# Weight sums of an MLP made in HBM instead of on VectorE, and begun two at a time behind loads in attention

## The chip, the cores and the metric

The kernel runs on one core of a Trainium2 chip. Its time is the device time of one execution in microseconds (us). Of the engines, TensorE (PE) multiplies matrices, VectorE (DVE) and ScalarE (ACT) work elementwise, GpSimd (POOL) works elementwise and issues DMAs of its own, and SyncE (SP) here only issues DMAs. Each of these takes its instructions strictly in program order; semaphores order them against each other.

## The reference

One layer of a decoder trunk on x of 1 x 512 x 1024 in float32: two token mixers side by side (a pooling mixer, and sparse attention with 16 heads of 64), merged by sigmoid gates and projected back, and then an MLP with a hidden width of 4096. The part that the change touches is the MLP:

```
x = x + mixers(rms_norm(x))                       # attention, pooling, gates, w_out
h = rms_norm(x)
x = x + square(relu(h @ w_ff1)) @ w_ff2           # 1024 -> 4096 -> 1024
out = rms_norm(x)
```

## The kernel before

The program is one long, unrolled sequence in three stages: input projections and attention (0 to some 370 us), the projection back (to some 460 us), and the MLP (to the end).

*The MLP.* The hidden width goes in four chunks of 1024 (c = 0 to 3). In a chunk there is a first product (layer 1, with `w_ff1`) and a second (layer 2, with `w_ff2`). Each is done with seven products of quarters in place of eight, after Winograd: a weight block falls into quarters A11, A12, A21, A22, and the weights that PE needs are A11, A12, A22 and four sums, S1 = A21 + A22, S3 = A11 + A21, S2 = S1 + A11 (first product) or S3 + A22 (second), and S4 = S2 + A12; the signs are in what they are multiplied with. Each block has two groups, g = 0 and 1, so that one weight is 128 x 1024 elements, 512 KB. Names carry layer, chunk and group: S2_231 is S2 of layer 2, chunk 3, group 1; S4_231 the S4 of the same.

*A weight's way.* SP loads it (`emit_load`, line 233) into one of five buffers `raw`; ScalarE rounds it to its upper part `wh` or `w3h` (line 304); VectorE makes the rest `wl` or `w3l` (line 306); PE multiplies in three combinations of upper and lower parts (line 1398 in the first product, line 1515 in the second). The second product's order of weights is A11 A11 S1 S1 S3 A12 S3 A12 A22 A22 S2 S4 S2 S4, groups in turn. A22 is added onto the banks of PSUM that held S3's product, once VectorE has taken that off into x (line 1539, two instructions for the two halves); so the first half of A22's first group waits for the first of the two, and its second half for the second.

*The sums.* Most sums are made in HBM before they are loaded: SP copies one quarter to a place in HBM (`make_sum`, line 263), and POOL issues a DMA that adds another quarter onto it (`add_sum`, line 271). Where a sum starts from another sum, the copy has to wait until that one's addition has landed; SP stands there, and the loads behind it too. The list `jobs` fixes the order of the sums. Before, one sum is begun behind each load from three loads behind the first phase on to the projection back, and behind every third load in the MLP (`sums_after`). The other sums are made on VectorE: a buffer is held, and the next weight is added onto it (line 316; line 294 for S4 of the second product). In the second product of chunks 0 to 2, S2 is S3 plus A22 on VectorE, for which S3's buffer is held until A22 is there. In chunk 3 both S2 and S4 are made in HBM.

*Attention.* POOL multiplies the attention weights P by a column sm (line 1078, tiles of 128x128 to 128x512), and PE then turns them (line 1095, result psT). The additions of sums that begin here stand among those on POOL. The "fillers" are the loads of the gate and projection weights that attention's matmuls are interleaved with.

Of the kernel before, what the change touches and what calls it, by code (L numbers as in the profile page):

```python
# [62 lines left out]
def trunk(ctx: ExitStack, tc: tile.TileContext, A, out):  # L63
# [41 lines left out]
    def add_key(k):  # L105
# [14 lines left out]
        else:  # L120
# [4 lines left out]
    P1 = ("ck ks u0 wk0 wk1 u1 wk2 u2 kw wk3 cv u3 V0 V1 V2 wv0 q0 wv1 ga0 wv2 wpool q1 wv3 ga1 q5 "  # L125
          "ga2 q2 pp0 q6 pp1 q7 pp2 q3 pp3 q4").split()
    FILL2 = "gb0 gb1 gb2 ga3 gb3 ga4 gb4 ga5 gb5 ga6 gb6 ga7 gb7".split()
# [8 lines left out]
    MLP0 = len(LD)  # L136
# [6 lines left out]
    jobs, late = [], []  # L143

    def quarters(layer, c, g):

        if layer == 2:
            return {f"{i + 1}{j + 1}": w_f2[1024 * c + 512 * j + 256 * g:1024 * c + 512 * j + 256 * g + 256,
                                            512 * i:512 * i + 512].rearrange("(k p) c -> p k c", p=128)
                    for i in range(2) for j in range(2)}  # L150
        o = 1024 * c + 512 * g
        return {f"{i + 1}{j + 1}": w_f1[512 * j:512 * j + 512, o + 256 * i:o + 256 * i + 256].rearrange(
            "(k p) c -> p k c", p=128) for i in range(2) for j in range(2)}

    def add_group(layer, c, g):

        q = quarters(layer, c, g)
        of = {"A" + k: v for k, v in q.items()}
        final = layer == 2 and c == LAST
        for o in ("S1", "S3", "S2", "S4")[:4 if final else 4 - layer]:  # L160
            of[o] = dp.tile(list(q["11"].shape), F32, name=f"{o}_{layer}{c}{g}")
        jobs.append((of["S1"], q["21"], q["22"]))
        jobs.append((of["S3"], q["11"], q["21"]))
        if late:
            jobs.append(late.pop())
        if layer == 1:
            late.append((of["S2"], of["S1"], q["11"]))
        if final:
            jobs.append((of["S2"], of["S3"], q["22"]))
            jobs.append((of["S4"], of["S2"], q["12"]))  # L170
        return of

    SUM_OF, PLUS = {}, {}
    SUMS = {"S2": "S4", "A12": "S4"}, {"S3": "S2", "A22": "S2", "S2": "S4"}

    def add_turn(layer, c, of, turn):
        for g, o in turn:
            key = f"{o}{layer}{c}{g}"
            to = SUMS[layer - 1].get(o) if "S4" not in of[g] else None
            if to:  # L180
# [10 lines left out]
    for c in range(4):  # L191
        of = [add_group(1, c, g) for g in range(2)]
        if c == 0:
            turn = [(g, o) for os in FIRST[:1] for o in os for g in range(2)]
            turn += [(g, o) for os in FIRST[1:] for g in range(2) for o in os]
        else:
            turn = [(g, o) for g in range(2) for o in IN_TURN]
        add_turn(1, c, of, turn)
        of = [add_group(2, c, g) for g in range(2)]
        seen = {}  # L200
        turn = []
        for o in OUT_TURN if c < LAST else [o for o in LAST_TURN for g in range(2)]:
            g = seen.get(o, 0)
            seen[o] = g + 1
            turn.append((g, o))
        add_turn(2, c, of, turn)
# [7 lines left out]
    def emit_load():  # L214

        i = st["load"]
        if i >= len(LD):
            return False
        segs = LD[i]
        a = segs[0][0].shape[1]  # L220
        b = sum(s.shape[2] for s, _ in segs)
        assert a * b <= 1024
        if not by_name() or st["kept"] < RAW:
            st["kept"] += by_name()
            t = wp.tile([128, 1024], F32, tag="raw", bufs=RAW, name=f"raw{i}")
        elif spare:
            t = spare.pop(0)
        else:
            return False
        st["load"] += 1  # L230
        v = t[:, :a * b].rearrange("p (a b) -> p a b", a=a)
        for s, o in segs:
            began = nc.sync.dma_start(v[:, :, o:o + s.shape[2]], s)
        raws[i] = (t, a, b)
        if sums_after(i):
            make_sum(began)
        if i >= len(P1) + len(FILL2) + 4 and (len(begun) > 2 or begun and st["sums"] == len(jobs)):
            add_sum()
        return True

    def sums_after(i):

        if i < MLP0:
            return len(P1) + 3 <= i < len(P1) + len(FILL2) + 8
        return i % 3 == 0

    def by_name():

        return st["load"] >= MLP0

    def give_back(*tiles):
        spare.extend(tiles)
        while spare and by_name() and emit_load():
            pass

    def make_sum(load):

        if st["sums"] < len(jobs):
            to, q, _ = jobs[st["sums"]]
            while any(q is jobs[n][0] for n in begun):  # L260
                add_sum()
            with tc.issue_after(load.ins):
                nc.sync.dma_start(to, q)
            begun.append(st["sums"])
            st["sums"] += 1

    def add_sum(behind=None):

        to, _, q = jobs[begun.popleft()]
        with tc.issue_after(behind.ins) if behind else nullcontext():  # L270
            POOL.dma_start(to, q, accum_op=ALU.add)  # L271
# [15 lines left out]
    def group_steps(i):  # L287

        key, at = WL[i]
        if i in PLUS:  # L290
            while st["load"] <= PLUS[i]:
                assert emit_load()
            t = raws.pop(PLUS[i])[0]
            DVE.tensor_tensor(t, t, held[key], op=ALU.add)
            give_back(held.pop(key))
            yield
        elif isinstance(at, str):
            t = held.pop(key)
        else:
            while st["load"] <= at:  # L300
                assert emit_load()
            t = raws.pop(at)[0]
# [134 lines left out]
    def fm_halves(keys, psp, posts, tag, xT):  # L437

        ws, ps = [], []
        for h in range(2):  # L440
            tok = slice(256 * h, 256 * h + 256)
            for i, k in enumerate(keys):
                if h == 0:
                    ws.append(use(k))
                    ps.append(psp.tile([128, S], F32, tag=tag[0], bufs=tag[1], name="psF"))
                prods = fm_products(ws[i][0], ws[i][1], xT, tok=tok)
                if h == 0:
                    prods = prods[0::3] + prods[2::3] + prods[1::3]
                for j, (a, b) in enumerate(prods):
                    last_mm[0] = PE.matmul(ps[i][:, tok], a, b, start=h == 0 and j == 0,  # L450
                                           stop=h == 1 and j == len(prods) - 1, skip_group_check=True)
                    if j % 12 == 11:
                        ahead()
                        step_side()
                if h == 1:
                    r = posts[i](ps[i])
                    if r is not None:
                        side.append(r)
                yield
# [91 lines left out]
    def evac0(i, after=None):  # L551
        sl = slice(128 * i, 128 * i + 128)
        for a in range(2):
            ks = slice(4 * a, 4 * a + 4)
            r = ACT.activation(hT[0][:, ks, sl], trs[i][a], AF.Copy)
            with behind(after) if after else nullcontext():
                v = DVE.tensor_tensor(hT[1][:, ks, sl], trs[i][a], hT[0][:, ks, sl].bitcast(F32), op=ALU.subtract)
        return r, v
# [8 lines left out]
    r, _ = evac0(1)  # L567
# [9 lines left out]
    first = fm_halves(("ck", "ks"), ps1, (lambda ps: first_posts[0](ps), lambda ps: first_posts[1](ps)), ("F", 2), hT)  # L577
# [95 lines left out]
    with ExitStack() as c1:  # L673
# [187 lines left out]
        for k in P1[2:]:  # L861
            i = int(k[-1]) if k[-1].isdigit() else None
# [710 lines left out]
    def out_of(t):  # L1573
        return MA[:, 2 * t:2 * t + 2, :].rearrange("p j c -> p (j c)")
# [48 lines left out]
    for f in range(2):  # L1623
        t = 2 + f
        o = out_of(t)
# [26 lines left out]
    o, r = out_of(3), sq[:, 3, 4:5]  # L1652
# [23 lines left out]
```

## Time and profile before

| | |
|---|---|
| time, median of 3 runs | 792.52 us (790.69 to 794.8) |
| the profiled execution | 793.79 us |
| its span, first to last instruction | 792.0 us |
| PE busy in the span | 774.8 us, 98% |
| VectorE, ScalarE, POOL busy | 619.3, 488.6, 179.5 us |
| loads of raw weights from w_ff | 54 |
| loads of sums, copies from w_ff, copies from a sum, additions | 44, 32, 12, 44 |

The profiled execution is one run; it stands 1.27 us above the median. A row of the timeline has the start in us, the duration, the engine, the line of the kernel, the operation, result <- operands by name, shape, and how many; in square brackets how long the engine had been idle before, and what ended that. An engine called SPq is SP's queue of DMA issues: the duration there is the issue, not the transfer. Matmuls of 512 columns are drawn 0.39 us long and start some 0.23 us apart, since PE's pipeline overlaps them.

### The profile page before, as it was taken

Reading aid. Unit: us, or ns where it says so; the run is one execution under the profiler, and the core shown is the slowest. Engines: PE = TensorE matmul, PEld = TensorE weight load, DVE = VectorE, ACT = ScalarE, POOL = GpSimd, SP = SyncE. Lnnn points to the kernel's source line nnn. Section 1 sums busy time; section 2 is a strip of 40 time slices with the busy share of each in tenths; the row PEclk is TensorE's granted clock in tenths of the full one; section 3 lists DMA queues with packets and bytes.
Section 4 is the critical chain, followed back from the end, with each engine's and each line's share of the span. In section 5 each row is a group of like instructions: output and inputs, shape, how many; then the busy total and the mean of one; then the engine's idle time right before and its main releaser. Section 6 shows DMA issues by size and latency. Waiting matters only on the chain. (4 is left out here: it accounts for less than half of the span.)

```text
span 792.0 us, 12823 instructions
## 1 busy us (share of the span) xinstructions
PE 774.8 (98%) x4541; PEld 674.1 (85%) x4541; DVE 619.3 (78%) x1177; ACT 488.6 (62%) x962; POOL 179.5 (23%) x245
## 2 busy tenths in 40 slices
PE   8999999999999999999999999999999999999995
PEld 6889877888888888988888899879997999789974
DVE  6888666445999888887656489997899789878897
ACT  6756543335988888896334485934783478247745
POOL 4000000025876666673100000111110110110002
PEclk9999999999999999999999999999999999999998
DMA  9554733487753434335956508989998996978552
GB/s 309 134 152 120 198 108 100 127 213 185 135 108 80 99 90 107 80 81 93 346 145 216 130 1 243 327 205 298 260 289 227 281 285 198 279 227 259 165 181 107
DMA packets 116154, 142.33 MB, mean 180 GB/s; under 512 B 5525, under 2 KB 88121, under 8 KB 115898
## 3 DMA queue, kind: packets, MB, share of 16 engines
q1 hardware_dynamic: 97690, 117.72, 45.8%
q0 software_dynamic: 18112, 23.07, 19.2%
q10 hardware_dynamic: 288, 0.72, 0.3%
q8 instruction: 36, 0.59, 0.3%
q14 instruction: 28, 0.23, 0.1%
HBM read 136.77 MB, written 48.23 MB: 234 GB/s over the span
## 5 line engine op out<-in xcount | busy, mean ns | idle before, releaser
L393 PE MATMUL psF<-R,wh 128*128 128x512 f32 x512 | 164.4, 402 | 0.0
L304 ACT ACTIVATE wh<-raw 128x1024 fp32r<-128x1024 f32 x75 | 79.2, 1058 | 85.7 <-PE psB L1515 32.1
L271 POOL DMA_DIRECT2D S<-w_ff x44 | 48.7, 1107 | 360.3 <-DMA S<-w_ff 286.1
L350 ACT ACTIVATE wh<-raw 128x512 fp32r<-128x512 f32 (+1 forms) x100 | 60.3, 620 | 85.3 <-PE psF L393 43.3
L306 DVE TENSOR_TENSOR wl<-raw,wh 128x1024 fp32r<-128x1024 f32 x75 | 92.2, 1231 | 23.4 <-ACT wh L304 23.4
L393 PEld LDWEIGHTS psF<-R,wh 128*128 128x128 f32 x512 | 92.1, 188 | 17.9
L393 PE MATMUL psF<-R,wl 128*128 128x512 f32 x256 | 101.3, 396 | 0.0
L1078 POOL TENSOR_SCALAR P<-P,sm,GT 128x128 f32<-128x128 f32 (+3 forms) x128 | 83.1, 671 | 55.2 <-DVE sm L1068 38.7
L352 DVE TENSOR_TENSOR wl<-raw,wh 128x512 fp32r<-128x512 f32 (+1 forms) x85 | 58.6, 696 | 26.3 <-ACT wh L350 26.2
L1062 ACT ACTIVATE P<-P,sm 128x128 f32<-128x128 f32 (+3 forms) x128 | 71.1, 559 | 9.9 <-DVE sm L1052 9.2
L1052 DVE CUSTOM_DVE_ANT_0 P<-psS,cst 128x128 f32<-128x128 f32 (+3 forms) x128 | 59.7, 483 | 8.4 <-PE psT L1095 5.3
L1398 PE MATMUL psB<-R,wh 128*128 128x256 f32 x352 | 64.1, 282 | 0.0
L304 ACT ACTIVATE w3h<-raw 128x1024 fp32r<-128x1024 f32 x37 | 39.1, 1055 | 36.3 <-PE psB L1398 14.1
L1110 DVE TENSOR_TENSOR PT<-psT,PT 128x512 fp32r<-128x512 f32 (+2 forms) x96 | 56.6, 596 | 3.5 <-ACT PT L1106 2.9
L393 PEld LDWEIGHTS psF<-R,wl 128*128 128x128 f32 x256 | 48.1, 188 | 11.3
L1106 ACT ACTIVATE PT<-psT 128x512 fp32r<-128x512 f32 (+2 forms) x96 | 49.5, 520 | 8.8 <-PE psT L1095 7.8
L1398 PEld LDWEIGHTS psB<-R,wh 128*128 128x128 f32 x352 | 54.3, 189 | 0.5 <-DVE R L1340 0.2
L306 DVE TENSOR_TENSOR w3l<-raw,w3h 128x1024 fp32r<-128x1024 f32 x37 | 45.8, 1238 | 9.2 <-ACT w3h L304 9.2
L1095 PE MATMUL psT<-ident,P 128*128 128x128 f32 x320 | 50.9, 273 | 0.9 <-DVE PT L1110 0.9
L1398 PE MATMUL psB<-R,wl 128*128 128x256 f32 x176 | 49.5, 281 | 0.0
L1095 PEld LDWEIGHTS psT<-ident,P 128*128 128x128 f32 x320 | 39.4, 140 | 9.7 <-issue 1.8
L1129 PE MATMUL psO<-PT,VV 128*128 128x256 f32 x320 | 47.7, 286 | 0.0
(381 smaller groups left out, 2001.8 us busy)
## 6 DMA issues: line engine op xcount, KB each, us to landing
raw<-w_ff SPq DMA_DIRECT2D x54, 512.0 KB, 6.1
S<-w_ff POOLq DMA_DIRECT2D x44, 512.0 KB, 7.5
raw<-S SPq DMA_DIRECT2D x44, 512.0 KB, 5.0
raw<-w_in SPq DMA_DIRECT2D x32, 512.0 KB, 4.1
S<-w_ff SPq DMA_DIRECT2D x32, 512.0 KB, 7.1
S<-S SPq DMA_DIRECT2D x12, 512.0 KB, 5.3
raw<-w_proj_nsa SPq DMA_DIRECT2D x8, 512.0 KB, 4.4
raw<-w_out SPq DMA_DIRECT2D x8, 512.0 KB, 4.5
```

The lines of the kernel that those rows point to most:

```text
L304: ACT.activation(h, t, AF.Copy)
L306: DVE.tensor_tensor(l, t, h.bitcast(F32), op=ALU.subtract)
L350: ACT.activation(h[:, sl], t[:, sl], AF.Copy)
L352: eng.tensor_tensor(l[:, sl], t[:, sl], h[:, sl].bitcast(F32), op=ALU.subtract)
L393: PE.matmul(ps, a, b, start=first and j == 0, stop=last and j == n - 1, skip_group_check=True)
L1052: DVE.tensor_tensor_reduce(out=P[:, o:o + n].rearrange("p (a c) -> p a c", c=128), in0=s, in1=m, scale=1.0, scalar=3e38, op0=ALU.add, op1= ...
L1062: last_exp[:] = [ACT.activation(c, c, AF.Exp, bias=sm[:, 0, e:e + 1], scale=-1.0, accum_out=sm[:, 1, e:e + 1])]
L1078: r = POOL.tensor_scalar(P[:, o:o + n], P[:, o:o + n], sm[:, 2, e:e + 1], GT[:, qb, c + e:c + e + 1], op0=ALU.mult, op1=ALU.mult)
L1095: PE.transpose(pt[:, 128 * j:128 * j + 128], P[:, 128 * j:128 * j + 128], ident)
L1106: ACT.activation(dH, src, AF.Copy)
L1110: DVE.tensor_tensor(dL, src, dH.bitcast(F32), op=ALU.subtract)
L1398: PE.matmul(out, w[u][:, k, 128 * f:128 * f + 128], XB[x][v][:, k, :], **kw)
```

## The change

Two edits. First, in the second product of chunks 0 to 2, S2 is no longer S3 plus A22 on VectorE but a sum made in HBM like the others (a copy of S3, to which A22 is added). There are 50 sums in HBM in place of 44; 18 of them are copies of another sum, in place of 12. Six additions at line 316 go, and six loads of raw weights come, since S2 has its own load. S3 and A22 are not held any longer. S4 of these products stays on VectorE. As in layer 1, S2 of a group stands in `jobs` one group later than its S3, by way of `late`.

Second, `sums_after` gives a number: from the tenth load behind the first phase to the fourth behind the last filler, two sums are begun behind each load. With it 26 sums are begun ahead of the MLP where 18 were, and 24 in the MLP where 26 were.

```diff
--- before.py
+++ after.py
@@ add_group @@
-        for o in ("S1", "S3", "S2", "S4")[:4 if final else 4 - layer]:
+        for o in ("S1", "S3", "S2", "S4")[:4 if final else 3]:
...
         if layer == 1:
             late.append((of["S2"], of["S1"], q["11"]))
+        if layer == 2:
+            late.append((of["S2"], of["S3"], q["22"]))
         if final:
-            jobs.append((of["S2"], of["S3"], q["22"]))
+            jobs.append(late.pop())
             jobs.append((of["S4"], of["S2"], q["12"]))
...
-    SUMS = {"S2": "S4", "A12": "S4"}, {"S3": "S2", "A22": "S2", "S2": "S4"}
+    SUMS = {"S2": "S4", "A12": "S4"}, {"S2": "S4"}
@@ emit_load @@
-        if sums_after(i):
+        for _ in range(sums_after(i)):
             make_sum(began)
@@ sums_after @@
-        if i < MLP0:
-            return len(P1) + 3 <= i < len(P1) + len(FILL2) + 8
-        return i % 3 == 0
+        first = len(P1) + len(FILL2)
+        if i < first + 8:
+            return (i >= len(P1) + 3) + (len(P1) + 10 <= i < first + 5)
+        return i >= MLP0 and i % 3 == 0
```

SP, in the second product of chunk 2, from the load of A11's second group on (`w_ff2` loads are quarters, `256x1x512` are copies of quarters, `16x8192` copies of sums). Before:

```order
L233 DMA raw65_4860<-w_ff2 128x2x512
L233 DMA raw67_4898<-S1_220_95 128x1024
L263 DMA S2_230_107<-S3_230_106 16x8192
L233 DMA raw64_4838<-S1_221_97 128x1024
L233 DMA raw66_4886<-S3_220_96 128x1024
L233 DMA raw5_4496<-w_ff2 128x2x512
L263 DMA S4_230_108<-S2_230_107 16x8192
L233 DMA raw65_4860<-S3_221_98 128x1024
L233 DMA raw67_4898<-w_ff2 128x2x512
L233 DMA raw64_4838<-w_ff2 128x2x512
L263 DMA S1_231_109<-w_ff2 256x1x512
```

and after:

```order
L235 DMA raw66_4908<-w_ff2 128x2x512
L266 DMA S3_231_116<-w_ff2 256x1x512
L235 DMA raw64_4860<-S1_220_99 128x1024
L235 DMA raw5_4518<-S1_221_102 128x1024
L235 DMA raw67_4920<-S3_220_100 128x1024
L266 DMA S2_231_117<-S3_231_116 16x8192
L235 DMA raw65_4882<-w_ff2 128x2x512
L235 DMA raw66_4908<-S3_221_103 128x1024
L235 DMA raw64_4860<-w_ff2 128x2x512
L266 DMA S4_231_118<-S2_231_117 16x8192
L235 DMA raw5_4518<-w_ff2 128x2x512
L235 DMA raw67_4920<-w_ff2 128x2x512
```

The last sums of the whole program, S3_231, S2_231 and S4_231, have moved here from the first product of chunk 3; the two loads behind S4_231's copy are A22's.

VectorE, in the second product of chunk 2, from the split of A22's first group on (`psB` are the products, the first two subtractions take S3's off). Before:

```order
L306 TENSOR_TENSOR wl64_4909<-raw64_4838,wh64_4908 128x1024
L1539 TENSOR_TENSOR x1_4485<-x1_4485,psB_7078 128x512
L316 TENSOR_TENSOR raw64_4838<-raw64_4838,raw66_4886 128x1024
L306 TENSOR_TENSOR wl65_4928<-raw5_4496,wh65_4927 128x1024
L1539 TENSOR_TENSOR x1_4485<-x1_4485,psB_7079 128x512
L316 TENSOR_TENSOR raw5_4496<-raw5_4496,raw65_4860 128x1024
L306 TENSOR_TENSOR w3l_4495<-raw64_4838,w3h_4494 128x1024
```

and after:

```order
L309 TENSOR_TENSOR wl64_4931<-raw5_4518,wh64_4930 128x1024
L1542 TENSOR_TENSOR x1_4507<-x1_4507,psB_7105 128x512
L1542 TENSOR_TENSOR x1_4507<-x1_4507,psB_7106 128x512
L309 TENSOR_TENSOR wl65_4950<-raw67_4920,wh65_4949 128x1024
L1542 TENSOR_TENSOR x1_4507<-x1_4507,psB_7016 128x512
L1542 TENSOR_TENSOR x1_4507<-x1_4507,psB_7017 128x512
L309 TENSOR_TENSOR w3l_4517<-raw65_4882,w3h_4516 128x1024
```

The two additions at line 316 are gone, and S3's second subtraction stands ahead of the split of A22's second group, where it stood behind it.

POOL, in attention, at the weights that its row 331.17 shows below. Before:

```order
L1078 TENSOR_SCALAR P_3795<-P_3795,sm_3794,GT_129 128x384
L1078 TENSOR_SCALAR P_3841<-P_3841,sm_3794,GT_129 128x384
L1078 TENSOR_SCALAR P_3858<-P_3858,sm_3857,GT_129 128x512
L1078 TENSOR_SCALAR P_3886<-P_3886,sm_3857,GT_129 128x512
L987 TENSOR_TENSOR cw_3810<-cw_3810,c8_3811 128x8x32
L1078 TENSOR_SCALAR P_3913<-P_3913,sm_3912,GT_129 128x384
```

and after:

```order
L1081 TENSOR_SCALAR P_3813<-P_3813,sm_3812,GT_135 128x384
L1081 TENSOR_SCALAR P_3859<-P_3859,sm_3812,GT_135 128x384
L274 DMA S1_211_90<-w_ff2 256x1x512
L1081 TENSOR_SCALAR P_3876<-P_3876,sm_3875,GT_135 128x512
L1081 TENSOR_SCALAR P_3904<-P_3904,sm_3875,GT_135 128x512
L990 TENSOR_TENSOR cw_3828<-cw_3828,c8_3829 128x8x32
```

The addition of S1_211 stands between two pairs of weights where there was none; its copy is the second behind one load on SP.

## Rows read from the trace of the kernel before

**Rows 1.** The page: busy time, two of its rows of 40 slices, one group.

```profile
PE 774.8 (98%) x4541; PEld 674.1 (85%) x4541; DVE 619.3 (78%) x1177; ACT 488.6 (62%) x962; POOL 179.5 (23%) x245
...
PEclk9999999999999999999999999999999999999998
DMA  9554733487753434335956508989998996978552
...
L271 POOL DMA_DIRECT2D S<-w_ff x44 | 48.7, 1107 | 360.3 <-DMA S<-w_ff 286.1
```

**Rows 2.** PE's waits, 420 to 792: us in total, times, longest.

```profile
PE psB L1515 <- DVE x L1539: 2.2, 2, 1.8
PE psB L1398 <- ACT wh L304: 0.6, 1, 0.6
```

**Rows 3.** Timeline of chunk 2, 685 to 689.

```profile
685.35 0.40 PE L1515 MATMUL psB<-wh,yT4H 128*128 128x512 f32 x1
...
685.78 1.06 ACT L304 ACTIVATE wh<-raw 128x1024 fp32r<-128x1024 f32 x1 [4.22 <-DMA raw<-w_ff]
...
686.52 0.40 PE L1515 MATMUL psB<-wh,yT4L 128*128 128x512 f32 x1
...
686.88 1.23 DVE L306 TENSOR_TENSOR wl<-raw,wh 128x1024 fp32r<-128x1024 f32 x1 [2.33 <-ACT wh L304]
688.02 0.68 DVE L1539 TENSOR_TENSOR x<-x,psB 128x512 f32<-128x512 f32 x1
...
688.75 0.50 PE L1515 MATMUL psB<-wh,yT4H 128*128 128x512 f32 x1 [1.84 <-DVE x L1539]
```

**Rows 4.** Timeline of chunk 0, the same place.

```profile
527.93 0.40 PE L1515 MATMUL psB<-wh,yT4L 128*128 128x512 f32 x1
...
528.66 0.50 PE L1515 MATMUL psB<-wh,yT4H 128*128 128x512 f32 x1 [0.33 <-DVE x L1539]
```

**Rows 5.** Groups by line: busy us, mean ns, idle before.

```profile
L316 DVE TENSOR_TENSOR raw<-raw,raw 128x1024 f32<-128x1024 f32 x14 | 17.1, 1221 | 0.2
```

**Rows 6.** Timeline of SP's issues: S3_230, two A11, S4_230, load, S3_231, S4_231.

```profile
632.85 0.55 SPq L263 DMA_DIRECT2D S<-w_ff  x1
...
642.75 4.07 SPq L233 DMA_DIRECT2D raw<-w_ff  x2
...
669.90 0.47 SPq L263 DMA_DIRECT2D S<-S  x1
670.47 0.52 SPq L233 DMA_DIRECT2D raw<-S  x1
...
685.00 0.57 SPq L263 DMA_DIRECT2D S<-w_ff  x1
...
715.37 0.50 SPq L263 DMA_DIRECT2D S<-S  x1
```

**Rows 7.** Line 233, the load issued at 670.47: issue to landing.

```profile
DMA to landing us min/median/max: 4.8/4.8/4.8
```

**Rows 8.** Timeline of ScalarE: its copy of that load.

```profile
675.39 1.06 ACT L304 ACTIVATE wh<-raw 128x1024 fp32r<-128x1024 f32 x1 [1.08 <-DMA raw<-S]
```

**Rows 9.** Line 233, the load issued at 659.71: issue to landing.

```profile
DMA to landing us min/median/max: 10.3/10.3/10.3
```

**Rows 10.** Timeline of attention, 330 to 341.

```profile
330.74 0.58 SPq L263 DMA_DIRECT2D S<-w_ff  x1
...
331.17 1.31 POOL L1078 TENSOR_SCALAR P<-P,sm,GT 128x384 f32<-128x384 f32 x2 [0.88 <-PE psT L1095]
...
335.35 1.54 POOL L1078 TENSOR_SCALAR P<-P,sm,GT 128x512 f32<-128x512 f32 x2 [2.87 <-DVE sm L1068]
...
340.52 0.60 PE L1095 MATMUL psT<-ident,P 128*128 128x128 f32 x4
```

**Rows 11.** Line 263, the copy issued at 330.74: issue to landing.

```profile
DMA to landing us min/median/max: 4.7/4.7/4.7
```

**Rows 12.** Line 263, the copy issued at 369.73: issue to landing.

```profile
DMA to landing us min/median/max: 8.5/8.5/8.5
```

## The prediction, as put on record before the run

> **What bounds the kernel now.** I read the page's busy and slice rows first, then PE's waits over the MLP, then the timeline around the longest of them, then SP's own issues, since the change is about what SP and POOL send.
>
> The page says PE: busy 774.8 us of a span of 792.0, at the full granted clock in all slices but the last [rows 1]. A change off PE pays only through PE's gaps. The waits view of 420 to 792 us, which is all of the MLP, is therefore the ceiling: its largest entry is 2.2 us for VectorE's subtraction of a product from the result (line 1539), and the next one is 0.6 [rows 2]. There is no other pool of time to win in this stage.
>
> The 2.2 us are two waits. The longer is in chunk 2. The first six matmuls of A22's first group start from 685.35 to 686.52, (686.52 - 685.35) / 5 = 0.234 apart; the seventh is due at 686.75 and starts at 688.75, with the releaser "DVE x L1539": 2.0 us lost [rows 3]. Why is that subtraction late? VectorE runs in program order. The subtraction at 688.02 stands behind the split of A22's second group (686.88, 1.23 us), and that split stands behind ScalarE's copy at 685.78, which had stood idle 4.22 us until its load landed. So a load that comes late delays a buffer of PSUM that has nothing to do with it. The same place in chunk 0 costs 0.5: 527.93 + 0.23 is 528.16, and the seventh starts at 528.66 [rows 4]. (The row books 0.33 of it, since the matmul before is drawn to its pipelined end.) In chunk 1 the waits show nothing at this place.
>
> **The change, part by part.**
>
> Six VectorE additions go (line 316, 1.22 us each, 14 before [rows 5] and 8 after). Their 7.3 us lie beside PE, which does not wait for them as such; by themselves they are worth 0. What they do to order is worth something. With S2 read from HBM, neither S3's nor A22's buffer is held for an addition, so A22 is loaded earlier, and on VectorE both subtractions of S3 now stand ahead of the split of A22's second group (the second fence of the change). The pair at 686.88 and 688.02 changes places, and the second subtraction needs nothing that is late. The stall of chunk 2 (2.0) and that of chunk 0 (0.5) should go: -2.5. From the other side: if A22 as a whole lands no earlier, its second half waits for its own weight instead, and 0 is won. I take -2.5, as the order rows show the exchange in all three chunks.
>
> Six more jobs are made in HBM: six more copies on SP, six more accumulating additions on POOL, and six more raw loads; in the MLP itself two sums fewer are begun (24 after, 26 before), since eight more are begun in attention. In the slices of the MLP the DMA engines are already at 0.5 to 0.99 [rows 1], so six loads more and two sums less are nearly a wash there. I price this at 0 by itself, and its bound through a late load below.
>
> *The new wait.* The sums come in one list, and the last of it is a chain: S3 of a group, S2 as a copy of S3, S4 as a copy of S2. SP cannot issue the copy of S2 before POOL's addition to S3 has landed, nor that of S4 before that to S2; while it waits, the loads behind it on SP wait too. Before, S3_231 is copied at 685.00 and S4_231 at 715.37, a chain of 30.37 us; the pair of the other group goes from 632.85 to 669.90, 37.05 us [rows 6]. Before, the second chain ends in the first product of chunk 3, where loads have time. After, the order of SP has S3_231 right behind the load of A11's second group in chunk 2, and S4_231 right ahead of the load of A22's first group (the first fence of the change). That A11 load is the second of the row at 642.75, which ends at 642.75 + 4.07 = 646.82 [rows 6]. With the 30.37 of the same chain, S4_231 goes out at 677.2, and the load behind it 0.57 later (669.90 to 670.47) at 677.8. The load at 670.47, which also follows an S4 copy, took 4.8 to land [rows 7], so A22 lands at 682.6. From landing to PE: 0.1 to ScalarE, which began on that load at 675.39 [rows 8] where 670.47 + 4.8 is 675.27; 1.10 from ScalarE's copy to VectorE's split (685.78 to 686.88), 1.14 to the subtraction behind it (to 688.02), 0.73 from there to PE (to 688.75) [rows 3]. Together 3.07. PE is ready at 685.35 and can start at 685.67: +0.3. With 37.05 in place of 30.37 it is 0.3 + 6.68 = 7.0. The other end is 0, since a chain of under 30.1 hides: the point from which it decides is a copy of S4_231 at 676.9. I take +0.3, as 30.37 is of the same sum, by the same three transfers, and keep 0 to 7.0.
>
> One row is against 4.8: the load at 659.71, the last that SP sends before it waits for POOL's addition to S2_230, took 10.3 [rows 9]. After the change, though, S4_231's addition can only begin once its copy has landed, about when the load has as well.
> The Trainium skill, page "DMA: Bandwidth & Descriptors", section "Issuing engines are not separate DMA queues", says that transfers begun by different engines share the same 16 DMA engines and get in each other's way. The 10.3 beside an addition agrees with it. Were A22's load to pay the same, it would land at 688.1, the stall would be 5.8 and the sum +3.3 in place of -2.2.
>
> *Attention.* Eight more sums are begun there, two behind one load. POOL issues their additions in program order among the attention weights, 1.1 us each (48.7 us for 44 [rows 1]), and an addition whose copy has not landed blocks POOL. The tight one is S1_211's (the third fence of the change): it stands ahead of the two 128x512 weights that POOL begins at 335.35, behind those that end at 331.17 + 1.31 = 332.48 [rows 10]. Its copy is the second behind the load, after the copy that goes out at 330.74, so about 0.6 later, at 331.3. The copy at 330.74 took 4.7 [rows 11]; two together I put at 6, which is an estimate from that row, so it lands at 337.3, and POOL comes to the weights 337.3 + 1.1 - 335.35 = 3.1 late. The first of them then ends 0.77 later (half of 1.54), and its turn on PE comes at 340.52 [rows 10]: 340.52 - 336.12 is 4.4 of slack. So 0. The bound is the copy issued at 369.73, which took 8.5 [rows 12]: it lands at 339.8, POOL is 5.6 late, and 1.2 of PE's time is lost; with the second weight and the 1.1 of a further addition behind it at most 2.3. The other seven additions have their copies one load earlier or more and cost 1.1 us of POOL each, inside the 2.87 it sat idle before 335.35 [rows 10]; a gain is excluded, since nothing is taken away there. I take 0, bounds 0 and 2.3.
>
> *Sum.* -2.5 + 0.3 + 0 = -2.2 against the profiled execution of 793.79 (span 792.0 and 1.79 around): 791.6. That execution is 1.27 above the median of 792.52, so against the median it is 790.3.
>
> **Rivals.**
>
> *A, the slower side: the wait moves to A22's first group.* The chain S3_231, S2_231, S4_231 takes more than 30.1 us where DMA is at nine tenths, SP stands on the copy of S4_231, and all loads behind it come late. For it: the pair of the other group needed 37.05 in the same part of a chunk, and now six loads more stand around it. Against it: 30.37 for the very sum. At 37.05 the sum is -2.5 + 7.0 = +4.5, 797.0; it is slower than before from a copy at 679.1 (a stall of 2.5), and beyond the bound of a measurement from about 683.1.
>
> *B: POOL blocks attention.* The copies behind one load take 8.5 and not 6, or several additions do so. For it: the one at 369.73 did; against it: DMA at three to seven tenths in most of attention's slices [rows 1]. Time: 790.3 + 2.3 = 792.6.
>
> *C: more is won than the waits show.* If PE's rows hide time, because matmuls are drawn to modelled ends, then taking VectorE and buffer holds away may shorten the MLP's pace: all waits of the MLP gone and the small excess between matmuls as well, 2 us more than forecast and then some, 788.0. Against it: matmuls of 512 columns start 0.23 to 0.24 apart wherever no wait is named [rows 3].
> The Trainium skill, page "Perfetto Trace Analysis", section "Identifying the Most-Contended Engine", warns that the matmul row's busy share is a poor measure and that of weight loads is better. Here weight loads are at 85% where matmuls are at 98%; by that there would be room of up to 15% on PE, of which the starts 0.23 apart show nothing.
>
> *D: nothing moves.* The copies of S2 land too late to free buffers earlier and the order on VectorE decides nothing: 792.5.
>
> **How the numbers follow.** The forecast (the stalls go, the chain just fits or costs under 2) has 0.52, A 0.28, B 0.08, C 0.08, D 0.04. About 0.5% (4.0 us) is what a measurement of this kernel can tell from no change. Forecast, B and D lie inside it. Of A, half lies over 796.5, since its stall goes up to 7.0 and more if a load takes the 10.3: 0.14. Of C all but a little is under 788.56: 0.07. So faster 0.07, same 0.79, slower 0.14. The range goes from C's 788.0 to A's 797.0; what is left out is under 2 in 10. The forecast's own range is 789.3 to 792.
>
> **What would show it.** Right: PE's waits for line 1539 (1542 now) fall from 2.2 to near 0; the subtractions of S3 in chunk 2 run one behind the other; SP's copy of S4_231 goes out by 677 and A22's first group starts without a wait for a weight. Wrong: a wait of PE for a weight's split in chunk 2's second product, with SP's copy of S4_231 standing 5 us or more ahead of it (A); POOL waiting for "DMA S" between 330 and 345 with PE's turns behind it (B); the pace of matmuls without waits below 0.23 (C). The prediction fails as a whole if the new sums make loads late in more than one place of a chunk.

## The result and the profile after

The changed kernel takes 800.31 us (median of 4 runs, 799.89 to 800.83) against 792.5 for the kernel before: a ratio of 1.0097, interval 1.007 to 1.0125. It is slower by 7.8 us, where 790.3 was forecast and 797.0 was the upper end. The profiled execution took 799.97, with a span of 798.2. One later run of the kernel before, out of 26, took 1540.51 us, a slow run that the ratios leave out.

The page of after, the rows that answer to [rows 1]:

```profile
PE 776.1 (97%) x4541; PEld 673.7 (84%) x4541; DVE 615.6 (77%) x1171; ACT 489.2 (61%) x962; POOL 184.7 (23%) x251
...
PEclk9999999999999999999999999999999999999998
DMA  9454733487774876674957508999999998854452
...
L274 POOL DMA_DIRECT2D S<-w_ff x50 | 56.3, 1126 | 336.7 <-DMA S<-w_ff 163.6
```

PE's work is the same, and so is its clock; VectorE has 3.7 us less. PE simply waits more. Its waits in the MLP (374 to 790; us in total, times, longest), which answer to [rows 2], and below the dots those in attention (170 to 374):

```profile
PE psB L1518 <- DVE wl L309: 3.8, 2, 2.1
PE psB L1518 <- DVE w3l L309: 0.9, 1, 0.9
PE psB L1401 <- ACT wh L307: 0.6, 1, 0.6
PE psB L1518 <- DVE yT3L L1456: 0.5, 1, 0.5
PE psB L1518 <- DVE x L1542: 0.5, 1, 0.5
...
PE psT L1098 <- DVE PT L1113: 2.3, 6, 0.7
PE psO L1123 <- DVE oT L1141: 1.1, 2, 0.6
PE psT L1098 <- DVE sm L1071: 0.4, 1, 0.4
PE psT L1098 <- POOL P L1081: 0.2, 1, 0.2
```

In attention before:

```profile
PE psO L1120 <- DVE oT L1138: 1.0, 2, 0.6
PE psT L1095 <- DVE PT L1110: 0.9, 4, 0.3
```

The wait for line 1539 (1542 now) fell from 2.2 to 0.5 in this execution, as forecast; in the second profile of the same kernel (a2) it is 1.7. In its place stand 4.7 us for the splits at line 309, one in each of the chunks 0, 1 and 2. In attention there are some 2 us more: 1.4 of line 1113 (1110 before) and 0.7 in three smaller entries. The table below has, for every run with a profile, the stretches that differ: attention is from PE's first matmul of the run of 72 at line 393 (169.15 before) to its first of the run of 321 that begins the projection back (374.40); c0 to c2 go from PE's first matmul of a chunk's second product to its first of the next chunk. Nothing else on PE's way from 374.40 on differs by more than 0.1 us, but for the last chunk of e2 (3.6 longer) and the first product of chunk 2 in e8 (0.7).

| kernel | attention | c0 | c1 | c2 | profiled run, us | median, us |
|---|---|---|---|---|---|---|
| before | 205.25 | 40.38 | 39.10 | 41.19 | 793.79 | 792.5 |
| b2, before again | 205.12 | 39.79 | 39.10 | 39.09 | 791.12 | 791.12 (1 run) |
| b3, before again | 205.23 | 40.40 | 40.07 | 39.01 | 792.24 | 792.24 (1 run) |
| after | 207.98 | 41.78 | 40.25 | 42.10 | 799.97 | 800.31 |
| a2, after again | 207.25 | 41.65 | 40.98 | 43.46 | 800.65 | 800.65 (1 run) |
| e1, VectorE's order | 208.35 | 40.64 | 39.08 | 43.16 | 799.05 | 795.16 |
| e2, one sum a load | 205.25 | 41.10 | 39.89 | 39.07 | 796.77 | 797.02 |
| e3, two sums alone | 207.63 | 40.05 | 39.11 | 39.04 | 792.76 | 794.23 |
| e4, open copies > 2 | 207.59 | 40.73 | 40.33 | 43.97 | 800.79 | 801.09 |
| e5, additions shifted | 206.15 | 42.26 | 40.38 | 44.52 | 800.91 | 800.31 |
| e6, e1 and S4_231 later | 208.12 | 39.78 | 39.05 | 39.02 | 793.15 | 793.44 |
| e7, e6 and e5 | 205.48 | 39.78 | 39.07 | 39.02 | 791.06 | 792.45 |
| e8, before, sums ahead | 205.16 | 39.78 | 39.10 | 39.47 | 791.62 | 791.62 |
| e9, e6, sums ahead | 205.24 | 40.22 | 39.05 | 39.01 | 791.07 | 791.17 |

A column's least value is what it takes without a stall: 205.1, 39.8, 39.1, 39.0. The stretches are those of the profiled run, which need not be a typical one: e1's is the second slowest of its ten runs, e7's the fastest of eleven. Between the first profiles of before and after, attention gives 2.7, the chunks 1.4 + 1.15 + 0.9, and the start of the kernel 0.2; together 6.3, the difference of PE's last matmuls (783.34 and 789.63). Against b2 and b3, whose last matmuls start at 780.65 and 781.76, the difference is 9.0 and 7.9; that of the medians is 7.8.

Where the 4.7 us are lost is seen in VectorE's rows of chunk 0, the stretch that ends S2 and S4 of the first group (timeline of after; ScalarE's copy of S4 is the row at 533.46):

```profile
532.07 1.22 DVE L297 TENSOR_TENSOR raw<-raw,raw 128x1024 f32<-128x1024 f32 x1
533.46 1.06 ACT L307 ACTIVATE wh<-raw 128x1024 fp32r<-128x1024 f32 x1 [2.56 <-DVE raw L297]
537.04 1.22 DVE L297 TENSOR_TENSOR raw<-raw,raw 128x1024 f32<-128x1024 f32 x1 [3.75 <-DMA raw<-w_ff]
538.18 0.68 DVE L1542 TENSOR_TENSOR x<-x,psB 128x512 f32<-128x512 f32 x1
538.78 1.22 DVE L309 TENSOR_TENSOR wl<-raw,wh 128x1024 fp32r<-128x1024 f32 x1
540.05 0.50 PE L1518 MATMUL psB<-wl,y22H 128*128 128x512 f32 x1 [1.69 <-DVE wl L309]
```

The first addition at line 297 makes S4 of the first group. Its upper part is done at 534.52, and the split could follow. Instead VectorE stands 3.75 us on the second addition, S4 of the *second* group, whose A12 has not landed. Only after that, and one subtraction, comes the split that PE waits for. VectorE stands in the same way in chunk 1 (2.94 us ahead of 617.23) and in chunk 2 (2.81 ahead of 699.23). Before, the addition of the second group stood behind that split:

```profile
535.46 1.22 DVE L306 TENSOR_TENSOR wl<-raw,wh 128x1024 fp32r<-128x1024 f32 x1
536.59 1.22 DVE L294 TENSOR_TENSOR raw<-raw,raw 128x1024 f32<-128x1024 f32 x1
```

So the change had moved a second pair of VectorE's instructions, a few rows below the pair that the prediction followed.

Those A12 come late because loads land later there. Issue to landing (least, median, most) of the loads issued from 519 to 527 before, and 522 to 529 after:

```profile
DMA to landing us min/median/max: 3.6/4.0/4.5
```

```profile
DMA to landing us min/median/max: 3.9/9.2/10.1
```

The four loads of after do not go out alone: from 522.11 to 529.92 SP sends five loads and two copies, where from 519.24 to 526.40 before it sent three and one. While they land, the DMA engines are busier than before (the last two numbers of a row are the DMA share and GB/s; before, then after):

```profile
526.00:534.00 8.00, 7.67 (x33) 5.95 (x33) 7.22 (x9) 2.69 (x3) 1.05 (x1) 1.00 0.74 214
529.00:537.00 8.00, 8.00 (x36) 6.51 (x35) 3.99 (x5) 3.18 (x3) 1.03 (x1) 1.00 1.07 378
```

S2 in HBM makes this and not the second sums in attention: at this place loads land in a median of 5.0 us in e3, which has only the second sums, and in 8.8 in e2, which has only S2.

The third loss is the wait for S4_231's copy that the prediction priced at 0.3. SP's issues in after, which answer to [rows 6], and PE's late start on A22:

```profile
652.29 0.57 SPq L266 DMA_DIRECT2D S<-w_ff  x1
...
669.62 0.50 SPq L266 DMA_DIRECT2D S<-S  x1
...
681.96 0.50 SPq L266 DMA_DIRECT2D S<-S  x1
682.54 1.05 SPq L235 DMA_DIRECT2D raw<-w_ff  x2
...
691.37 0.47 PE L1518 MATMUL psB<-wh,yT4H 128*128 128x512 f32 x1 [0.48 <-DVE x L1542]
```

The chain from S3_231 to S4_231 took 29.67 (30.37 forecast), and PE lost 0.64, start to start: 691.37 is 0.87 behind the matmul before it, where 0.23 is the pace. In the second profile of the same kernel it lost 1.8.

In attention POOL stands on the addition of S1_211 (compare 335.35 in [rows 10]). Its row names VectorE, but the copy that it needs, issued at 331.50, landed at 338.51, just ahead of it. Most of PE's loss comes ten microseconds later (timeline of after, then the same places of before):

```profile
339.06 1.08 POOL L274 DMA_DIRECT2D S<-w_ff  x1 [6.45 <-DVE PT L1113]
339.72 1.96 POOL L1081 TENSOR_SCALAR P<-P,sm,GT 128x512 f32<-128x512 f32 x2
...
348.53 2.01 POOL L274 DMA_DIRECT2D S<-w_ff  x1
348.68 3.52 DVE L941 TENSOR_TENSOR R<-oT,R 128x256 fp32r<-128x256 f32 x2
349.22 2.69 POOL L355 TENSOR_TENSOR wl<-raw,wh 128x512 fp32r<-128x512 f32 x1
352.69 0.39 DVE L941 TENSOR_TENSOR R<-oT,R 128x256 fp32r<-128x256 f32 x1
...
353.83 0.41 PE L1098 MATMUL psT<-ident,P 128*128 128x128 f32 x2 [0.70 <-DVE PT L1113]
```

```profile
348.08 1.29 POOL L352 TENSOR_TENSOR wl<-raw,wh 128x512 fp32r<-128x512 f32 x1
348.55 1.44 DVE L938 TENSOR_TENSOR R<-oT,R 128x256 fp32r<-128x256 f32 x2
```

The weights that began at 335.35 begin at 339.72. That alone costs PE 0.4 us. Then the issue of an addition stands right ahead of POOL's split. The split begins later than before and takes 2.69 in place of 1.29, and VectorE's two additions of 128x256 beside it take 3.52 us in place of 1.44. VectorE's turn for PE is late from there on: at 353.83 PE is 1.0 behind the same matmul of before, and 2.2 behind at 357.21 (0.2 of either is from the kernel's start). The pair takes 2.5 to 3.5 in the six profiles that have an addition's issue right ahead of that split (after, a2, e1, e3, e4, e6) and 1.4 in the eight that have none. The same six have POOL's earlier wait of 4.8 to 6.5 us, so whether the split is late by that wait or by its neighbour is not separated.

### The profile page after: what moved, and what is told of

It reads as the page before. It is cut to its first block, busy times and chain, and to the rows that moved or that the text cites. A ratio compares the mean times of both kernels' runs of the same rounds, so it can differ in the third digit from the quotient of the medians.

```text
span 798.2 us, 12862 instructions
## 1 busy us (share of the span) xinstructions
PE 776.1 (97%) x4541; PEld 673.7 (84%) x4541; DVE 615.6 (77%) x1171; ACT 489.2 (61%) x962; POOL 184.7 (23%) x251
## 5 line engine op out<-in xcount | busy, mean ns | idle before, releaser
L274 POOL DMA_DIRECT2D S<-w_ff x50 | 56.3, 1126 | 336.7 <-DMA S<-w_ff 163.6
L1081 POOL TENSOR_SCALAR P<-P,sm,GT 128x128 f32<-128x128 f32 (+3 forms) x128 | 85.0, 728 | 42.3 <-DVE sm L1071 30.9
L307 ACT ACTIVATE w3h<-raw 128x1024 fp32r<-128x1024 f32 x37 | 39.1, 1056 | 36.1 <-PE psB L1401 14.3
```

Source lines behind the costliest of these rows:

```text
L307: ACT.activation(h, t, AF.Copy)
L1081: r = POOL.tensor_scalar(P[:, o:o + n], P[:, o:o + n], sm[:, 2, e:e + 1], GT[:, qb, c + e:c + e + 1], op0=ALU.mult, op1=ALU.mult)
```

## The experiments

Each ran in five rounds beside the kernel before, with 4 to 12 runs of its own, except the three last, which are one profiled run each. Behind a median stand the least and the most.

**e1, VectorE's order.** The addition for S4 is queued behind the split that precedes it in program order.

```diff
-            DVE.tensor_tensor(t, t, held[key], op=ALU.add)
+            with tc.issue_after(last_split[0].ins):
+                DVE.tensor_tensor(t, t, held[key], op=ALU.add)
...
-        DVE.tensor_tensor(l, t, h.bitcast(F32), op=ALU.subtract)
+        last_split[0] = DVE.tensor_tensor(l, t, h.bitcast(F32), op=ALU.subtract)
```

> The changed kernel, with one edit: on VectorE the addition that makes S4 (line 297 of the changed kernel) is queued behind the split made just before it in program order, so that S4 of the second group no longer stands ahead of the split of S4 of the first group. Theory 1 (the loss in the MLP is VectorE's order: it stands on the second group's addition, whose A12 lands late, while the first group's split is ready behind it): the three waits of PE for a split of S4 in chunks 0, 1 and 2 (1.9, 1.1 and 2.2 us from start to start) go, all or nearly; time 795.1 to 796 against 800.3. Rival 2 (the loads are late as such, whatever stands where): the waits move on to S2 or S4 of the second group, the MLP keeps its 3.5 us over before; time 799 to 800.5.

795.16 (793.29 to 799.5), ratio to before 1.0047 [1.0031, 1.0064]. PE's waits from 374 on:

```profile
PE psB L1519 <- DVE x L1543: 2.6, 1, 2.6
PE psB L1402 <- ACT wh L308: 0.7, 1, 0.7
PE psB L1519 <- DVE yT3L L1457: 0.5, 1, 0.5
PE psB L1519 <- DVE wl L310: 0.4, 1, 0.4
```

The three waits for S4's splits are gone (the 0.4 is at another weight, in chunk 0). The median falls by 5.15, or by 4.5 if each kernel is taken against its own runs of before (7.8 over and 3.3 over), through one edge of order and with the same transfers: theory 1. New is that PE waits 2.6 us at A22 in this execution, and that the ten runs spread over 6 us where 21 of before spread over 2.5.

**e2, S2 in HBM with one sum behind each load.**

```diff
-            return (i >= len(P1) + 3) + (len(P1) + 10 <= i < first + 5)
+            return int(i >= len(P1) + 3)
```

> The changed kernel with S2 in HBM, but with one sum begun behind each load in attention, as before (18 begun ahead of the MLP and 32 in it). Theory 1 (attention loses 2.7 us to POOL, which stands 6.5 us on the addition of S1_211 ahead of two attention weights): attention is as before, PE's first matmul of the projection back starts at 374.5 and not 377.3; the order of VectorE in the MLP is the same, so its waits stay; 797.6, or up to 2 more where the eight sums put off to the MLP slow its loads. Rival 2 (attention loses by something other than the second sum): 800 or more.

797.02 (794.21 to 800.04), 1.0067 [1.0046, 1.0087]. Attention is as before (205.25): the second sums cost it all of its 2.7. The waits for S4's splits stay in chunks 0 and 1, at 0.9 and 0.75. With eight sums fewer ahead, the last chain reaches chunk 3: SP's copy of S4_231 goes out at 751.13 and holds up the loads of S2. PE waits 2.2 us there, the granted clock is 0.59 over the 4.2 us behind the wait (758.0 to 762.2), and the last chunk's second product is 3.6 longer.

**e3, the kernel before with two sums behind a load.** Its `sums_after` and its loop in `emit_load` are those of the change.

> The kernel before, with only the second part of the change: two sums begun behind each load from the tenth filler on, and S2 of the second product still on VectorE. Theory 1 (the second part alone costs attention 2.7, and the MLP is touched little): 794.5 to 796 against 792.5. Rival 2 (what stands behind the second addition matters, and here it is another sum, or the waits are made by the six S2 sums): 792 to 793.

794.23 (792.12 to 795.64), 1.0026 [1.0015, 1.0036]. Attention takes 2.4 more than before. So the second part of the change alone is a loss, with S2 still on VectorE: 2.35 against its own runs of before, inside the 2 to 3.5 expected. In its profile c2 has no stall. The two parts nearly add up: 2.35 here and 5.1 in e2, against 7.8 for both.

**e4, additions put off by a count.**

```diff
-            if i % 4 == 3 and len(begun) > 1:
+            if i % 4 == 3 and len(begun) > 2:
```

> The changed kernel with one edit: in attention POOL begins an addition only when more than two copies are open, in place of more than one, so that each addition stands one place later and its copy has had longer to land. The number of sums, copies and additions is the same. Theory 1 (POOL's wait for a copy that has not landed is the loss): attention's 2.7 us go, 797.6. Rival 2 (eight more additions of 1.1 us on POOL, or twice the transfers, are the loss by their number): 800 as after.

801.09 (798.95 to 805.59), 1.0118 [1.0097, 1.0139]. That is rival 2's time, but the run does not tell the theories apart, since the edit missed its aim. POOL's waits from 300 to 375 show that it still stands, 4.8 and 4.2 us. The rows name VectorE, but each addition begins 0.55 us after its copy has landed (337.26 and 358.80). S2_111's addition came to stand where S1_211's had been:

```profile
POOL S L274 <- DVE c L988: 4.8, 1, 4.8
POOL S L274 <- DVE sm L1071: 4.2, 1, 4.2
```

**e5, additions put behind the weights of two steps later.**

```diff
-            if i % 4 == 3 and len(begun) > 1:
+            if i > 3 and i % 4 == 1 and len(begun) > 1:
```

> The changed kernel with one edit in attention: POOL's additions are queued behind the weights of two steps later, so that the addition of S1_211 stands behind the two 128x512 weights that it held up, and no addition stands where its copy has not landed. Number of sums, copies and additions as in the changed kernel; VectorE's order in the MLP as there. Theory 1 (POOL's wait for the copy of S1_211, and the backlog behind it, make attention's loss): of attention's 2.7 us less than 0.8 are left; 797.5 to 798.5. Rival 2 (the eight additions as such: while POOL issues one and does the split behind it, VectorE's additions of 128x256 take 2.1 us in place of 0.4, wherever POOL stands): 1.5 or more are left; 799 to 800.5.

800.31 (799.33 to 800.91), 1.0107 [1.0093, 1.0121]. The time expected was missed, and the attention expected was met nearly: 0.9 over before with the same eight additions, in place of 2.7. Rival 2, which left 1.5 or more, is out: the two additions of 128x256 take 1.4 here, as before. What attention gave, the MLP of this execution took: c0 to c2 add up to 127.2, against 124.1 in after. One part of that is new. In chunk 2 PE waits 2.34 us for the split of S4, and then the granted clock falls to half (1.2 GHz) for some 3 us (windows: us, busy of PE, PEld, DVE, ACT, POOL, clock, DMA share, GB/s):

```profile
700.00:701.50 1.50, 0.00 (x0) 0.00 (x0) 1.50 (x3) 1.06 (x1) 0.00 (x0) 1.00 0.03 11
702.00:706.00 4.00, 4.00 (x13) 3.14 (x12) 2.44 (x3) 0.40 (x1) 0.00 (x0) 0.62 0.73 247
706.50:710.00 3.50, 3.50 (x16) 2.82 (x16) 2.58 (x4) 1.23 (x2) 0.00 (x0) 1.00 0.66 202
```

Matmuls that start 0.23 apart at the full clock start 0.43 apart there (703.23, 703.66, 704.09), so the stall of 2.5, start to start, costs 1.7 more.

**e6, e1 with S4_231's copy begun later.** The last sum is passed over twice, so it goes out six loads later.

```diff
+        if st["sums"] == len(jobs) - 1 and st.setdefault("put_off", 0) < 2:
+            st["put_off"] += 1
+            return
```

> The changed kernel with VectorE's order mended as in e1_s4_behind, and the copy of S4_231 begun six loads later than there, so that SP does not stand on it ahead of A22's loads in chunk 2. Theory 1 (that wait is rival A of the prediction: 0.5 us in the changed kernel's profiled run, 2.7 in that of e1_s4_behind, and the cause of e1's spread from 793.3 to 799.5): the wait of PE at A22's first group in chunk 2 goes, and most of the spread; 793.5 to 794.5. Rival 2 (the loads of A22 are late because the DMA engines are full, not because SP stands): the wait stays, 795 with the same spread.

793.44 (792.82 to 795.42), 1.0023 [1.0013, 1.0034]. The wait at A22 is gone (c2 39.02), the spread falls from 6.2 to 2.6, and 1.7 us of e1's median with it (1.9 if each is taken against its own runs of before). Theory 1: SP's stand on a copy was rival A of the prediction, and most of e1's spread goes with it.

**e7, the three edits together (e1, e6, e5).**

> The changed kernel with the three edits together: VectorE's order (e1), S4_231's copy later (e6), POOL's additions two steps later in attention (e5). If the three losses are separate and each edit removes its own: attention as before or 0.8 over it, the MLP 1 to 2.5 us under before; 790 to 792, level with before or just under it. If what is left comes from the six loads more in a full MLP: 793 to 795.

792.45 (791.06 to 793.92), 1.0002 [0.9991, 1.0012]: level with before, and 0.45 over the top of the 790 to 792 expected. Over its own runs of before, after was 7.8, e1 3.3, e6 1.4 and e7 0.4: each of the three edits takes a part, and together they take nearly all. PE's waits from 374 on, and then the landing times of its loads in chunk 0 (issued from 519.4 to 526):

```profile
PE psB L1405 <- ACT wh L311: 0.6, 1, 0.6
PE psB L1522 <- DVE yT3L L1460: 0.5, 1, 0.5
PE psB L1522 <- ACT w3h L311: 0.2, 1, 0.2
```

```profile
DMA to landing us min/median/max: 3.3/9.3/10.2
```

The loads are as slow as in after, 9.3 against 9.2, and in this profile PE does not wait for one of them. Late loads are the condition of the loss in the MLP; VectorE's order is what made it a loss.

**e8, the kernel before with more sums ahead, in the projection back.**

```diff
-        return i % 3 == 0
+        return 2 if i < MLP0 + 4 else i % 3 == 0
```

> The kernel before, with S2 on VectorE as before and attention as before; but behind each of the first four loads of the MLP, which SP sends while PE still does the projection back, two sums are begun, in place of one behind every third load: six sums more ahead of the MLP. Theory (what helped the MLP of e3_two_sums, 2.5 us less there in the profiled runs, is that fewer sums are made while the MLP's loads need the DMA engines; in attention the same sums cost 2.4): the two waits for line 1539 go and nothing is lost; 789.5 to 790.5. Rival (SP stands on the copies of S2 or the sums crowd out the first product's loads at 470): 792 or more.

791.62 (790.09 to 792.83), 0.9997 [0.9988, 1.0006]: no difference to before. The two waits are absent from its profile (0.7 and 0.4 of the table stand at other places), but the time is not 789.5. That put the size of the waits in before in doubt; b2 and b3 are for that.

**e9, e6 with sums ahead in the projection back in place of attention.**

```diff
-            return (i >= len(P1) + 3) + (len(P1) + 10 <= i < first + 5)
-        return i >= MLP0 and i % 3 == 0
+            return int(i >= len(P1) + 3)
+        return 2 if MLP0 <= i < MLP0 + 4 else i >= MLP0 and i % 3 == 0
```

> The changed kernel with VectorE's order mended (e1) and the copy of S4_231 begun later (e6), with one sum behind each load in attention as before the change, and two sums behind each of the first four loads of the MLP, which SP sends during the projection back. If what the change loses in attention comes from its second sums alone, and the MLP needs only that sums are ahead of it and VectorE's order is right: attention as before (374.5), MLP as in e7 (406.1 from the start of the projection back to PE's last matmul, in place of 408.9); 789.5 to 791.5 against 792. Rival: S2_231 now stands two loads nearer to A22's first load in chunk 2, and SP's wait for it takes the place of the one for S4_231; 793 or more.

791.17 (790.71 to 792.98), 0.999 [0.998, 1.0]. It is the fastest of the versions, inside the range expected: 9 us under the changed kernel, with S2 in HBM, and 0.8 under before, at the edge of what the interval tells from nothing.

**b2 and b3, the kernel before again.** No edit.

> The kernel before, unchanged, for a second profile. If the 2.0 us stall at A22 of chunk 2 belongs to every execution, it stands here too. If the gain of 2.5 us was read from an execution that had more of a wait than most (its 793.79 is 1.7 over the median of 26 runs, 792.05), the stall is 0 to 1 us here, and the whole some 1 to 2 us shorter.

> The kernel before, unchanged, for a third profile; as b2_before_again.

791.12 and 792.24. PE's waits of b2 from 374 on:

```profile
PE psB L1398 <- ACT wh L304: 0.6, 1, 0.6
PE psB L1515 <- DVE yT3L L1453: 0.5, 1, 0.5
PE psB L1515 <- ACT w3h L304: 0.2, 1, 0.2
```

There is no wait for line 1539 in b2, and one of 0.7 in b3, in chunk 1. The stall of 2.0 belonged to one execution.

**a2, the changed kernel again.** No edit.

> The changed kernel, unchanged, for a second profile. If the losses found belong to the program and not to one execution: PE waits 4 to 6 us in all for splits of S4's first group in chunks 0 to 2, attention ends its last matmul before the projection back 2.4 to 3 us later than before, and A22's first group in chunk 2 waits between 0 and 3 us.

800.65. The two longest of PE's waits from 374 on:

```profile
PE psB L1518 <- DVE wl L309: 3.6, 3, 2.2
PE psB L1518 <- DVE x L1542: 1.7, 1, 1.7
```

PE's waits for splits of S4 are 1.16, 1.83 and 2.38 us from start to start, 5.4 in all; A22 waits 1.8; attention takes 2.0 more than before, less than the 2.4 to 3 expected. The losses belong to the program; how much falls on each varies.

## Why the prediction was wrong

- *The step that failed* is the reading of VectorE's new order, behind the term of -2.5. It followed one exchanged pair, S3's subtraction and A22's split (686.88 and 688.02), and let that stand for all that the change does to the order. The same change put S4 of the second group ahead of the split of S4 of the first, and the sum has no term for that. After's order shows it four rows behind the end of the second fence of the change. From start to start it cost 1.86, 1.06 and 2.23 us in after, 5.15 in all, and 5.4 in a2; e1 takes the three waits away with that edge alone, and its median is 5.15 lower.
- *Six loads more are a wash*: right in itself (e7 has them and no stall), wrong as a term of 0. They make loads land in 9 us where 4 were, and the order above turns that into a wait. The prediction looked at the DMA slices as a price, bounded it by a late load at A22 alone, and not by what waits behind other loads. Its own last sign, that it fails as a whole if loads come late in more than one place, is what came.
- *The gain of 2.5* was read from one execution, 1.3 us over the median and 1.7 over the median of 26 later runs (792.05). Over the stall-free 117.9, c0 to c2 hold 2.8 in that one, 0.1 in b2 and 1.6 in b3. A wait that comes and goes with the execution is worth its mean. The mechanism was right, and the stalls do go (e6, e7), but b2 has the same numbers without the change, so the median had less than 2.5 to give.
- *The wait of SP at S4_231*, +0.3 within 0 to 7.0: the right place and the right chain (29.67 for 30.37). It was 0.64 and 1.8 in two executions of after, 1.2 in e5, 2.3 in e4 and 2.7 in e1. Its price is larger than its length when the clock falls behind it, as in e1 and e4 (1.4 and 1.6 more). Two of rival A's thresholds are 0.3 early by the prediction's own sum: a stall of 2.5 goes with a copy at 679.4, and one of 6.5 with 683.4.
- *Attention*, 0 within 0 to 2.3: the direct wait came out as bounded. The copy issued at 331.50 took 7.0 (6 was put in), POOL was 4.4 late, and PE's first turn lost 0.4. What was missed comes ten microseconds later, where an addition's issue and POOL's late split fall on VectorE's pair of additions. The loss is 2.0 to 3.1 in six profiles with the wait, 0.2 and 0.9 in the two where those weights stand ahead of the addition (e7, e5), and 0 with one sum a load (e2, e9).
- *The rivals.* A and B both came in part, together with the loss that none of the cases held. C and D did not: no pace below 0.23, no time of 792.5.
- *Removed work was worth nothing*, as costed: 7.3 us of VectorE's additions are gone, and e7 is level with before.

That the range ended at 797.0 follows from this: it held each of the waits that had been thought of, but one at a time.

## What to carry to other kernels

When a change moves instructions under a scheduler, compare the whole order of the engine that feeds the bound one, through the whole period, and ask of each exchanged pair which of the two can be late; one edge of order was worth 5 us here, while the 7.3 us of VectorE's work that the change removed were worth nothing. Take the size of a stall from several executions, or from the spread of the times. Begin transfers ahead in a stage that does not wait for the engine that issues them: in attention the second sums cost 2.4 us (e3), and six of them begun during the projection back cost nothing (e8, e9).

## What the runs showed of the hardware

VectorE's addition of two operands from SBUF does not run freely beside POOL's split of 128x512. Two of 128x256 took 3.52 us beside an addition's issue and a split, and 1.44 beside a split alone, against 0.39 for one alone in the same rows. They end by the split: in after the pair ends at 348.68 + 3.52 = 352.20, which is 0.3 after POOL's split ends (349.22 + 2.69 = 351.91). In every one of the 14 profiles one of the two additions ends 0.28 to 0.29 us after that split, whether the split took 1.3 or 2.7.
The Trainium skill, page "SBUF — State Buffer", section "SBUF: two separate sides", says that these two engines share a pair of ports that one instruction holds to its end while the other is blocked. The rows agree; the ports themselves stand in no row.

The clock: PE's waits of 2.14 us in e4, 2.25 in e2, 2.34 in e5 and 2.58 in e1 were followed by some 3 to 4 us with a granted clock of 0.50 to 0.62 (the full clock is 1.00, the lower level 1.2 GHz). After waits of 2.06 in after and 2.21 in a2, both in chunk 2, it stayed at 1.00. So the length of the wait alone does not tell whether the clock falls; what else decides stays open. Why e5's median is not below that of after, though attention is 1.8 shorter in its profile, stays open too; its MLP stalls were longer in the one execution seen.
